# Turning square blocks on VectorE in place of 128x128 transposes on TensorE, in a two-layer decoder trunk

## The chip, the cores and the metric

The kernel runs on one core of a Trainium2 chip. The metric is the device time of one execution in microseconds (us); the number compared is the median of three runs. The profile comes from one further execution, read from the hardware profiler. Five engines work side by side on a core: TensorE (PE; its weight loads are listed as PEld), VectorE (DVE), ScalarE (ACT), GpSimd (POOL) and SyncE (SP), which here only issues transfers.

## The reference, cut to what matters

The input x has 256 tokens of 2048 features, in float32. Two layers follow each other, each a mixer and a feed-forward part, with plain residuals:

```python
h = x
hn = rmsnorm(h, norm_mix[0]);  h = h + s5_mixer(hn, ...)        # state-space mixer, GELU, gated linear unit
hn = rmsnorm(h, norm_ffn[0]);  h = h + swiglu(hn, ...)          # d_ff = 5632
hn = rmsnorm(h, norm_mix[1]);  h = h + sliding_window_attention(hn, ...)
hn = rmsnorm(h, norm_ffn[1]);  h = h + swiglu(hn, ...)
out = rmsnorm(h, norm_final)

def swiglu(x, w_gate, w_up, w_down):
    return (jax.nn.silu(x @ w_gate) * (x @ w_up)) @ w_down
```

A matrix product contracts over features. TensorE contracts over the partitions of its operands. So whatever enters a product as the left operand (the residual h, and the gated values of the feed-forward part) has to be turned first: tokens stand on the partitions where it is computed, and features must stand there where it is used.

## The kernel before, in words

**Products in three parts.** A float32 product is made of three matmuls in a reduced format. Each operand is split into a high part and a low part (the rest), and `products` (L922 to L924) multiplies high by high, high by low and low by high. A `piece` is 512 rows of a weight matrix by 512 columns for both halves of the tokens: 4 x 2 x 3 = 24 matmuls of 128x512. `linear` runs four pieces (2048 features in) or two or three pieces (the down product).

**Weights.** Each piece needs one weight tile of 1 MB. SP's queue loads it into `raw` (two buffers), ScalarE writes its high part (L122), and VectorE its low part (L127). `Weights.next` prepares the tile of two pieces ahead when a piece starts. There are three tiles for split weights, so the high part of piece i+2 can be written when TensorE is done with piece i-1. A `raw` buffer is free, and its next load can start, when the low part is written.

**The residual.** `h` is two tiles of 128 tokens by 2048 features. `Norm.chunk` is called when a chunk of 512 features of h is final; it squares the chunk for the norm and puts a closure into the list `left`. `linear` and `glu` take closures out of that list after each piece, so the turning of a chunk lies among the pieces of the next product.

**Turning.** `normed` turns a chunk of h: eight 128x128 transposes on TensorE into PSUM (L966), then for each of four pairs an activation that scales and writes the high part (L969) and a VectorE instruction for the low part (L970). In `swiglu`, `turned` does the same for a chunk of gated values `act`: eight transposes (L1061), then two casts (L1063) and two subtractions (L1064). There are three norms of h with four chunks each, and two feed-forward parts with eleven chunks of gated values each. The feed-forward part works in groups of chunks: `gu(c)` computes a chunk with eight pieces (four for the gate, four for up), and `down(g)`, twelve pieces for a group of three, comes one chunk later.

**Order.** Engines work through their instructions in the order in which a scheduler put them when the program was built. An engine that waits holds up all that stands behind it in its own list.

Of the kernel before, what the change touches and what calls it, by code (L numbers as in the profile page):

```python
# [17 lines left out]
P = 128  # L18
# [38 lines left out]
def kernel(  # L57
# [9 lines left out]
    def nm(s):  # L67
        uid[0] += 1
        return f"{s}_{uid[0]}"
# [14 lines left out]
    def turned_tile(name):  # L84
        return pp.tile([P, 2, 4, T], F32R, tag="b8", name=nm(name))

    def normed_tile(name):
        return wp.tile([P, 2, 4, T], F32R, tag="xt", name=nm(name), bufs=4)


    class Weights:
        def __init__(self):
            self.src, self.raw, self.hl = [], [], []
            self.early = {}
            self.third = None
            self.used = 0
            self.limit = 0
# [861 lines left out]
    def normed(n, g):  # L959

        o = normed_tile("xT")
        for a in range(4):
            kt = 4 * n + a
            pt = bank([P, 2, P], "tr")
            for t in range(2):
                PE.transpose(pt[:, t], h[t][:, kt * P : (kt + 1) * P], ident)  # L966
            v = pt.rearrange("p t c -> p (t c)")
            gc = gcol[:, g, kt : kt + 1]
            S.activation(o[:, 0, a], v, AF.Copy, scale=gc)  # L969
            V.scalar_tensor_tensor(o[:, 1, a], v, gc, o[:, 0, a].bitcast(F32), ALU.mult, ALU.subtract)  # L970
        return o

    class Norm:


        def __init__(self, g):
            self.g = g
            ssq = wp.tile([P, 32], F32, tag="ssq", name=nm("ssq"), bufs=2)
            self.ssq = ssq[:, : 2 * NCH].rearrange("p (t n) -> p t n", t=2)
            self.xt = [None] * NCH  # L980

        def square(self, n, t):
            junk = wp.tile([P, 512], F32, tag="junk", name=nm("junk"), bufs=2)
            S.activation(
                junk, h[t][:, 512 * n : 512 * n + 512], AF.Square, accum_out=self.ssq[:, t, n : n + 1]
            )

        def chunk(self, n, t):
            self.square(n, t)
            if t == 1:  # L990
                left.append(lambda: self.xt.__setitem__(n, normed(n, self.g)))

        def scale(self):
# [4 lines left out]
    class Last(Norm):  # L998


        def chunk(self, n, t):
            if n == 0 and t == 0:
                self.w = pp.tile([P, D], F32, tag="b8", name="nf")
                nc.scalar.dma_start(self.w, norm_final.unsqueeze(0).to_broadcast([P, D]))
                warm = wp.tile([P, 1], F32, name="warm")
                tc.keep_in_program_order(S.activation(warm, ident[:, 0:1], AF.Sqrt))
            self.square(n, t)
            hc = h[t][:, 512 * n : 512 * n + 512]
# [8 lines left out]
            a, b = slice(0, D // 2), slice(D // 2, D)  # L1017
            V.tensor_scalar(h[t][:, a], h[t][:, a], r, None, ALU.mult)
            nc.sync.dma_start(out[rows, a], h[t][:, a])
            S.activation(h[t][:, D // 2 : D - 512], h[t][:, D // 2 : D - 512], AF.Copy, scale=r)  # L1020
            V.scalar_tensor_tensor(hc, hc, r, wc, ALU.mult, ALU.mult)
            nc.scalar.dma_start(out[rows, b], h[t][:, b])

    def tmp2(name, bufs=4):
        return wp.tile([P, 512], F32, tag=name, name=nm(name), bufs=bufs)

    def glu(norm):
        def load_h(c):
            for t in range(2):
                cs = slice(512 * c, 512 * c + 512)  # L1030
                tc.keep_in_program_order(nc.sync.dma_start(h[t][:, cs], x[t * P : (t + 1) * P, cs]))

        for c in range(NCH):
            left.append(partial(load_h, c))
            if c == 0:
                pa, pb = accs
                for _, half, q in G_ORDER[EARLY:8]:
                    piece(accs[half], gt[q], q == 0, q == 3)
                    if left:
                        left.pop(0)()  # L1040
            else:
                pa = linear(gt)
                pb = linear(gt)
            for t in range(2):
                hc = h[t][:, 512 * c : 512 * c + 512]
                sg = tmp2("act")
                S.activation(sg, pb[t], AF.Sigmoid)
                V.tensor_tensor(sg, pa[t], sg, op=ALU.mult)
                V.tensor_tensor(hc, hc, sg, op=ALU.add)
                norm.chunk(c, t)  # L1050

    def swiglu(norm, out_norm):
        ht = {}
        r = [None]

        def turned(c, hm):
            o = turned_tile("hT")
            for t in range(2):
                pt = bank([P, 4, P], "tr")
                for a in range(4):  # L1060
                    PE.transpose(pt[:, a], hm[t][:, a * P : (a + 1) * P], ident)  # L1061
                ts_ = slice(t * P, (t + 1) * P)
                S.copy(o[:, 0, :, ts_], pt)  # L1063
                V.tensor_tensor(o[:, 1, :, ts_], pt, o[:, 0, :, ts_].bitcast(F32), op=ALU.subtract)  # L1064
            ht[c] = o

        def gu(c):
            pg = linear(norm.xt)
            if r[0] is None:
                r[0] = norm.scale()  # L1070
            sg = []
            for t in range(2):
                s = tmp2("act")
                S.activation(s, pg[t], AF.Silu, scale=r[0][:, t : t + 1])  # L1074
                sg.append(s)
            pu = linear(norm.xt)
            for t in range(2):
                V.scalar_tensor_tensor(sg[t], pu[t], r[0][:, t : t + 1], sg[t], ALU.mult, ALU.mult)
            left.append(lambda: turned(c, sg))

        def down(g):
            xt = Later(ht, FF_GROUPS[g])
            for n in range(NCH):
                last = out_norm.g is None and g == len(FF_GROUPS) - 1 and n == NCH - 1
                acc = linear(xt, len(FF_GROUPS[g]), halves=last)
                for t in range(2):
                    hc = h[t][:, 512 * n : 512 * n + 512]
# [13 lines left out]
    def attention(norm, out_norm):  # L1101
        with tc.tile_pool(name="at", bufs=1) as ap:
# [119 lines left out]
            for c in range(4):  # L1222
                acc = linear(norm.xt)
                b = bias(c)
                tc.keep_in_program_order(S.mul(b, b, HD ** -0.5))
                q = ap.tile([P, 2, 512], F32, tag="q", name=nm("q"), bufs=2)
                for t in range(2):
                    V.scalar_tensor_tensor(q[:, t], acc[t], r8[:, t : t + 1], b, ALU.mult, ALU.add)
                turn_q, scores, turned_s, values = heads(c, q)
                slots.append([turn_q, *late[:1], partial(scores, 0)])  # L1230
                slots.append([*late[1:], partial(scores, 1)])
                slots.append([partial(turned_s, 0)])
                slots.append([partial(values, 0)])
                late = [partial(turned_s, 1), partial(values, 1)]
# [8 lines left out]
            for n in range(NCH):  # L1243
                acc = accs[n] if n < 2 else linear(ot, 4)
                for t in range(2):
                    hc = h[t][:, 512 * n : 512 * n + 512]
                    V.tensor_tensor(hc, hc, acc[t], op=ALU.add)
                    out_norm.chunk(n, t)

# [20 lines left out]

# [27 lines left out]
```

## Time and profile before

| | before |
|---|---|
| median of 3 runs | 2014.27 us (2013.39 to 2014.71) |
| the profiled execution, its own time | 2014.75 us |
| its span in the trace | 2013.0 us |
| TensorE matmuls, busy | 1971.2 us, 98% of the span |
| TensorE weight loads, busy | 1633.5 us, 81% |
| VectorE busy | 1087.0 us, 54% |
| ScalarE busy | 857.9 us, 43% |
| mean busy share of the DMA engines, by stage | 0.54 to 0.68 |

The busy time of an engine is the time in which at least one of its instructions runs. Matmuls overlap at their ends, so a stream of matmuls that start 0.23 us apart and last 0.39 us each counts as fully busy. The 1.75 us between the profiled execution's time and its span lie outside the trace.

### The profile page before, as it was taken

Reading aid. Unit: us, or ns where it says so; the run is one execution under the profiler, and the core shown is the slowest. Engines: PE = TensorE matmul, PEld = TensorE weight load, DVE = VectorE, ACT = ScalarE, POOL = GpSimd, SP = SyncE. Lnnn points to the kernel's source line nnn. Section 1 sums busy time; section 2 is a strip of 40 time slices with the busy share of each in tenths; the row PEclk is TensorE's granted clock in tenths of the full one; section 3 lists DMA queues with packets and bytes.
Section 4 is the critical chain, followed back from the end, with each engine's and each line's share of the span. In section 5 each row is a group of like instructions: output and inputs, shape, how many; then the busy total and the mean of one; then the engine's idle time right before and its main releaser. Section 6 shows DMA issues by size and latency. Waiting matters only on the chain.

```text
span 2013.0 us, 25105 instructions
## 1 busy us (share of the span) xinstructions
PE 1971.2 (98%) x10640; PEld 1633.5 (81%) x10640; DVE 1087.0 (54%) x1343; ACT 857.9 (43%) x871; POOL 103.4 (5%) x77
## 2 busy tenths in 40 slices
PE   7699999999999999999999999999999999999998
PEld 6577888888888888888888888888888888888886
DVE  8964555444444454454566885544454445444445
ACT  6554444333334333433455554433333343343333
POOL 6850000000000000000000000000000000000000
PEclk9899999999999999999999999999999999999999
DMA  4037665565566565555554435566556555655564
GB/s 129 23 109 230 202 202 190 188 188 188 188 189 190 190 198 192 190 188 188 181 196 159 151 126 169 188 189 190 192 192 198 188 188 189 190 190 192 192 198 146
DMA packets 183316, 360.62 MB, mean 179 GB/s; under 512 B 10402, under 2 KB 10466, under 8 KB 183076
## 3 DMA queue, kind: packets, MB, share of 16 engines
q1 hardware_dynamic: 182192, 355.56, 54.8%
q8 instruction: 83, 1.36, 0.3%
q10 hardware_dynamic: 580, 2.14, 0.3%
q0 software_dynamic: 432, 1.33, 0.2%
q14 instruction: 29, 0.24, 0.0%
HBM read 356.90 MB, written 2.10 MB: 178 GB/s over the span
## 4 chain that ended last, share of the span: by engine, by line
PE 93%; DVE 5%; DMA 1%; ACT 1%; issue 0%; POOL 0%; DVEq 0%; ACTq 0%
PE acc L922 29%; PE acc L924 29%; PE acc L923 29%; DVE scan L573 1%; PE tr L1061 1%; DVE V L578 1%; DVE V L576 1%; DMA raw<-in_s_w_glu_dram 1%; DVE w L127 1%; PE pv L210 1%; PE tr L966 1%; PE tr L1196 1%; PE py L798 0%; PE at L1166 0%; PE px L210 0%
## 5 line engine op out<-in xcount | busy, mean ns | idle before, releaser
L127 DVE TENSOR_TENSOR w<-raw,w 128x2048 fp32r<-128x2048 f32 x330 | 757.1, 2294 | 826.3 <-ACT w L122 826.2
L122 ACT ACTIVATE w<-raw 128x2048 fp32r<-128x2048 f32 x332 | 636.2, 1916 | 983.2 <-PE acc L924 834.1
L922 PE MATMUL acc<-w,xT 128*128 128x512 f32 x1568 | 613.1, 391 | 0.0
L924 PE MATMUL acc<-w,xT 128*128 128x512 f32 x1568 | 610.5, 389 | 0.0
L923 PE MATMUL acc<-w,xT 128*128 128x512 f32 x1568 | 610.2, 389 | 0.0
L922 PEld LDWEIGHTS acc<-w,xT 128*128 128x128 f32 x1568 | 294.4, 188 | 62.6 <-issue 2.3
L924 PEld LDWEIGHTS acc<-w,xT 128*128 128x128 f32 x1568 | 294.3, 188 | 61.5
L923 PEld LDWEIGHTS acc<-w,xT 128*128 128x128 f32 x1568 | 294.5, 188 | 60.3
L922 PE MATMUL acc<-w,hT 128*128 128x512 f32 x704 | 275.2, 391 | 0.0
L923 PE MATMUL acc<-w,hT 128*128 128x512 f32 x704 | 273.6, 389 | 0.0
L924 PE MATMUL acc<-w,hT 128*128 128x512 f32 x704 | 273.4, 389 | 0.0
L922 PEld LDWEIGHTS acc<-w,hT 128*128 128x128 f32 x704 | 132.2, 188 | 28.1 <-ACT hT L1063 1.2
L924 PEld LDWEIGHTS acc<-w,hT 128*128 128x128 f32 x704 | 132.1, 188 | 27.6
L923 PEld LDWEIGHTS acc<-w,hT 128*128 128x128 f32 x704 | 132.2, 188 | 27.0
L923 PE MATMUL acc<-w,gt 128*128 128x512 f32 x256 | 99.8, 390 | 0.6 <-DVE w L127 0.6
L922 PE MATMUL acc<-w,gt 128*128 128x512 f32 x256 | 100.1, 392 | 0.0
L924 PE MATMUL acc<-w,gt 128*128 128x512 f32 x256 | 99.7, 389 | 0.0
L923 PEld LDWEIGHTS acc<-w,gt 128*128 128x128 f32 x256 | 48.1, 188 | 10.8 <-DVE w L127 1.0
L1088 DVE TENSOR_TENSOR h<-h,acc 128x512 f32<-128x512 f32 x64 | 43.5, 687 | 24.4 <-PE acc L924 24.4
L924 PEld LDWEIGHTS acc<-w,gt 128*128 128x128 f32 x256 | 48.1, 188 | 10.0
L922 PEld LDWEIGHTS acc<-w,gt 128*128 128x128 f32 x256 | 48.1, 188 | 9.9
L1074 ACT ACTIVATE act<-acc,ry 128x512 f32<-128x512 f32 x44 | 30.1, 690 | 59.9 <-PE acc L924 59.9
(242 smaller groups left out, 1204.6 us busy)
## 6 DMA issues: line engine op xcount, KB each, us to landing
raw<-in_ffn_w_gate_dram SPq DMA_DIRECT2D x88, 1024.0 KB, 5.2
raw<-in_ffn_w_up_dram SPq DMA_DIRECT2D x88, 1024.0 KB, 5.2
raw<-in_ffn_w_down_dram SPq DMA_DIRECT2D x88, 1024.0 KB, 5.1
raw<-in_s_w_glu_dram SPq DMA_DIRECT2D x32, 1024.0 KB, 5.3
raw<-in_attn_w_qkv_dram SPq DMA_DIRECT2D x20, 1024.0 KB, 5.1
raw<-in_attn_w_o_dram SPq DMA_DIRECT2D x16, 1024.0 KB, 5.0
xk<-in_x_dram SPq DMA_DIRECT2D x4, 512.0 KB, 7.1
h<-in_x_dram SPq DMA_DIRECT2D x8, 256.0 KB, 5.8
```

Source lines behind the costliest of these rows:

```text
L122: keep(S.activation(w[:, 0], self.raw[i], AF.Copy))
L127: keep(e.tensor_tensor(lo, self.raw[i], hi.bitcast(F32), op=ALU.subtract))
L210: return (lambda *a, **k: pin(f(*a, **k))) if self.on else f
L573: keep(V.tensor_tensor(t_, ws[..., part], bc(Vt[hf][:, k - 1, :, part], 1, 2), op=ALU.mult))
L576: V.tensor_tensor(v, v, t_[:, 0], op=ALU.add)
L578: V.tensor_tensor(v, v, t_[:, 1, ::-1], op=ALU.add)
L922: keep(PE.matmul(acc, x_[:, 0], w[0][:, a], start=first, stop=False))
L923: PE.matmul(acc, x_[:, 0], w[1][:, a], start=False, stop=False)
L924: PE.matmul(acc, x_[:, 1], w[0][:, a], start=False, stop=last)
L966: PE.transpose(pt[:, t], h[t][:, kt * P : (kt + 1) * P], ident)
L1074: S.activation(s, pg[t], AF.Silu, scale=r[0][:, t : t + 1])
L1088: V.tensor_tensor(hc, hc, acc[t], op=ALU.add)
```

## The change

The residual becomes one tile laid out as [128, chunk, half of the tokens, 512], and the two gated tiles of a chunk become one tile [128, 2, 512]. With that, a chunk is turned by VectorE: `blocks_turned` takes 32 partitions of a chunk (32 tokens of each half) and makes four transposes of 32x32 blocks, each of which writes to another quarter of the partitions of a new tile `bt`. Four calls, 16 VectorE instructions over 32 partitions x 256 elements, turn a chunk. A last closure, `split`, makes the high and low parts from `bt`. For gated values it is one activation and one subtraction over 1024 elements; for h it is four pairs over 256 elements, as before but read from `bt`.

This holds for chunks 0 to 2 of the norm behind the mixer of layer 0 and of the norm behind the attention (`Norm(0, (0, 1, 2))`, `Norm(2, (0, 1, 2))`), and for chunks 0 to 9 of the gated values in each of the two feed-forward parts. Chunk 3 of those two norms, all four chunks of the norm ahead of the attention, and chunk 10 of the gated values are still turned by TensorE. The tile `q` in the attention has one buffer in place of two.

```diff
+    def block_tile():
+        return wp.tile([P, 4, T], F32, tag="bt", name=nm("bt"), bufs=1)
+
+    def blocks_turned(o, v, tb):
+        src = v[32 * tb : 32 * tb + 32].rearrange("p t (a c) -> p t a c", a=4)
+        dst = o.rearrange("p a (t k) -> p t a k", t=2)
+        for q in range(4):
+            V.transpose(dst[32 * q : 32 * q + 32, :, :, 32 * tb : 32 * tb + 32],
+                        src[:, :, :, 32 * q : 32 * q + 32])
...
         def chunk(self, n, t):
             self.square(n, t)
-            if t == 1:
+            if t == 1 and n in self.blocks:
+                o, v = normed_tile("xT"), block_tile()
+                self.xt[n] = o
+                left.extend(partial(blocks_turned, v, h[:, n], tb) for tb in range(4))
+
+                def split():
+                    gc = gcol[:, self.g, 4 * n : 4 * n + 4]
+                    for a in range(4):
+                        S.activation(o[:, 0, a], v[:, a], AF.Copy, scale=gc[:, a : a + 1])
+                        V.scalar_tensor_tensor(o[:, 1, a], v[:, a], gc[:, a : a + 1], o[:, 0, a].bitcast(F32),
+                                               ALU.mult, ALU.subtract)
+
+                left.append(split)
+            elif t == 1:
                 left.append(lambda: self.xt.__setitem__(n, normed(n, self.g)))
...
         def gu(c):
+            last = c == FF_GROUPS[-1][-1]
...
             pu = linear(norm.xt)
             for t in range(2):
-                V.scalar_tensor_tensor(sg[t], pu[t], r[0][:, t : t + 1], sg[t], ALU.mult, ALU.mult)
-            left.append(lambda: turned(c, sg))
+                V.scalar_tensor_tensor(sg[:, t], pu[t], r[0][:, t : t + 1], sg[:, t], ALU.mult, ALU.mult)
+            if last:
+                left.append(lambda: turned(c, sg))
+                return
+            o, v = turned_tile("hT"), block_tile()
+            ht[c] = o
+            left.extend(partial(blocks_turned, v, sg, tb) for tb in range(4))
+
+            def split():
+                S.activation(o[:, 0], v, AF.Copy)
+                V.tensor_tensor(o[:, 1], v, o[:, 0].bitcast(F32), op=ALU.subtract)
+
+            left.append(split)
...
-                q = ap.tile([P, 2, 512], F32, tag="q", name=nm("q"), bufs=2)
+                q = ap.tile([P, 2, 512], F32, tag="q", name=nm("q"))
...
-    h = [wp.tile([P, D], F32, name=f"h{t}") for t in range(2)]
+    h = wp.tile([P, NCH, 2, 512], F32, name="h")
...
-    n0 = Norm(0)
+    n0 = Norm(0, (0, 1, 2))
...
-    n2 = Norm(2)
+    n2 = Norm(2, (0, 1, 2))
```

What stands in the engines' lists is shown at three places, with the rows of before first and those of the change second.

The first place is VectorE behind the up product of one chunk of gated values. `act` is the tile of gated values, written last by L1078 before and by L1102 now; `w` is the low part of a weight tile, and `hT` the low part of the turned chunk.

```order
L1078 SCALAR_TENSOR_TENSOR act_3317<-acc_3320,ry_3307,act_3317 128x512
L127 TENSOR_TENSOR w_3441<-raw_3382,w_3441 128x2048
L127 TENSOR_TENSOR w_3485<-raw_3411,w_3485 128x2048
L1064 TENSOR_TENSOR hT_3470<-tr_3471,hT_3470 128x4x128
L1064 TENSOR_TENSOR hT_3470<-tr_3478,hT_3470 128x4x128
L127 TENSOR_TENSOR w_3514<-raw_3444,w_3514 128x2048
```

```order
L1102 SCALAR_TENSOR_TENSOR act_3586<-acc_3590,ry_3317,act_3586 128x512
L982 STREAM_TRANSPOSE bt_3710<-act_3586 32x2x4x32 x4
L127 TENSOR_TENSOR w_3713<-raw_3652,w_3713 128x2048
L982 STREAM_TRANSPOSE bt_3710<-act_3586 32x2x4x32 x9
L127 TENSOR_TENSOR w_3750<-raw_3681,w_3750 128x2048
L982 STREAM_TRANSPOSE bt_3710<-act_3586 32x2x4x32 x3
L1112 TENSOR_TENSOR hT_3709<-bt_3710,hT_3709 128x1024
L127 TENSOR_TENSOR w_3787<-raw_3716,w_3787 128x2048
```

Sixteen transposes now stand around the next two low parts, and one subtraction of 1024 elements stands in place of two of 512.

The second place is VectorE at the end of the attention, where the chunks 0 and 1 of h become final one after the other (`h`, L1247 before, L1282 now) and are turned for the second feed-forward part (`xT` is the low part of a turned chunk of h).

```order
L1247 TENSOR_TENSOR h_2217<-h_2217,acc_8686 128x512
L1247 TENSOR_TENSOR h_2218<-h_2218,acc_8687 128x512
L127 TENSOR_TENSOR w_9174<-raw_9105,w_9174 128x2048
L127 TENSOR_TENSOR w_9224<-raw_9134,w_9224 128x2048
L970 SCALAR_TENSOR_TENSOR xT_9203<-tr_9204,gcol,xT_9203 128x256
...
L127 TENSOR_TENSOR w_9274<-raw_9177,w_9274 128x2048
```

```order
L1282 TENSOR_TENSOR h<-h,acc_8735 128x512
L1282 TENSOR_TENSOR h<-h,acc_8736 128x512
L982 STREAM_TRANSPOSE bt_9216<-h 32x2x4x32 x4
L127 TENSOR_TENSOR w_9227<-raw_9154,w_9227 128x2048
L982 STREAM_TRANSPOSE bt_9216<-h 32x2x4x32 x6
L127 TENSOR_TENSOR w_9272<-raw_9183,w_9272 128x2048
L1012 SCALAR_TENSOR_TENSOR xT_9215<-bt_9216,gcol,xT_9215 128x256 x4
L982 STREAM_TRANSPOSE bt_9224<-h 32x2x4x32 x8
L127 TENSOR_TENSOR w_9317<-raw_9230,w_9317 128x2048
L982 STREAM_TRANSPOSE bt_9224<-h 32x2x4x32 x8
L127 TENSOR_TENSOR w_9362<-raw_9275,w_9362 128x2048
L1012 SCALAR_TENSOR_TENSOR xT_9223<-bt_9224,gcol,xT_9223 128x256 x4
```

Behind these rows come the addition to h for chunk 2, a low part, ten transposes of chunk 2, a low part and the last six transposes. So three chunks are turned here in two products.

The third place is TensorE in the gated linear unit of layer 0, between the first and the second piece of the second column chunk (`gt` is the turned output of the mixer, `tr` the PSUM tile of a transpose).

```order
L923 MATMUL acc_2351<-w_2280,gt_1731 128x512
L924 MATMUL acc_2351<-w_2280,gt_1731 128x512
L966 MATMUL tr_2382<-ident,h_2217 128x128
L966 MATMUL tr_2382<-ident,h_2218 128x128
...
L966 MATMUL tr_2397<-ident,h_2218 128x128
L922 MATMUL acc_2350<-w_2309,gt_2119 128x512
```

```order
L924 MATMUL acc_2350<-w_2279,gt_1731 128x512
L922 MATMUL acc_2351<-w_2279,gt_1731 128x512
L923 MATMUL acc_2351<-w_2279,gt_1731 128x512
L924 MATMUL acc_2351<-w_2279,gt_1731 128x512
L922 MATMUL acc_2350<-w_2308,gt_2119 128x512
```

The eight transposes between two pieces are gone, and matmul follows matmul. The same holds at 25 other places.

## Rows read from the trace of the kernel before

**Rows 1.** Chain of work that ended last: share of the span by engine.

```profile
PE 93%; DVE 5%; DMA 1%; ACT 1%; issue 0%; POOL 0%; DVEq 0%; ACTq 0%
```

**Rows 2.** Busy time by engine in one stretch, TensorE's clock, DMA share, GB/s.

```profile
348.63:393.08 44.45, 44.45 (x203) 36.88 (x201) 20.97 (x12) 17.55 (x12) 0.00 (x0) 1.00 0.60 189
```

**Rows 3.** The page's costliest groups: busy, mean ns | idle before, and its releaser.

```profile
L127 DVE TENSOR_TENSOR w<-raw,w 128x2048 fp32r<-128x2048 f32 x330 | 757.1, 2294 | 826.3 <-ACT w L122 826.2
L122 ACT ACTIVATE w<-raw 128x2048 fp32r<-128x2048 f32 x332 | 636.2, 1916 | 983.2 <-PE acc L924 834.1
```

**Rows 4.** Timeline of TensorE around one turned chunk: start, us, engine, line.

```profile
348.24 0.40 PE L924 MATMUL acc<-w,xT 128*128 128x512 f32 x1
348.47 1.04 PE L1061 MATMUL tr<-ident,act 128*128 128x128 f32 x8
349.26 0.47 PE L922 MATMUL acc<-w,xT 128*128 128x512 f32 x1
349.58 0.39 PE L923 MATMUL acc<-w,xT 128*128 128x512 f32 x1
```

**Rows 5.** Chain that ended last, in order of time: the turned chunks.

```profile
348.63 0.87 PE tr L1061 x8
393.08 0.88 PE tr L1061 x8
...
481.94 0.87 PE tr L1061 x8
591.63 0.87 PE tr L1061 x8
```

**Rows 6.** Timeline of the first turned chunk of h, TensorE, VectorE and ScalarE.

```profile
168.13 0.39 PE L924 MATMUL acc<-w,gt 128*128 128x512 f32 x1
...
171.56 0.48 PE L922 MATMUL acc<-w,gt 128*128 128x512 f32 x1
...
170.68 2.28 DVE L127 TENSOR_TENSOR w<-raw,w 128x2048 fp32r<-128x2048 f32 x1
...
178.46 1.92 ACT L122 ACTIVATE w<-raw 128x2048 fp32r<-128x2048 f32 x1 [2.96 <-DMA raw<-in_s_w_glu_dram]
```

**Rows 7.** Groups by form, VectorE and ScalarE: the nearest to what is new.

```profile
L970 DVE SCALAR_TENSOR_TENSOR xT<-tr,gcol,xT 128x256 fp32r<-128x256 f32 x48 | 19.9, 476 | 2.0 <-ACT xT L969 2.0
L1216 DVE TENSOR_TENSOR oT<-po,oT 128x256 fp32r<-128x256 f32 x16 | 6.1, 409 | 0.0
L1187 DVE TENSOR_SCALAR sc<-sc,sm 128x256 f32<-128x256 f32 x32 | 11.2, 349 | 0.0
L1064 DVE TENSOR_TENSOR hT<-tr,hT 128x512 fp32r<-128x512 f32 x44 | 28.2, 682 | 0.0
L210 ACT ACTIVATE U<-xk 128x1024 f32<-128x1024 f32 x4 | 4.3, 1082 | 0.0
```

**Rows 8.** Timeline of VectorE and ScalarE behind one chunk of gated values.

```profile
1318.46 1.43 DVE L1078 SCALAR_TENSOR_TENSOR act<-acc,ry,act 128x512 f32<-128x512 f32 x2 [0.52 <-PE acc L924]
1321.08 2.29 DVE L127 TENSOR_TENSOR w<-raw,w 128x2048 fp32r<-128x2048 f32 x1 [1.20 <-ACT w L122]
1326.53 2.29 DVE L127 TENSOR_TENSOR w<-raw,w 128x2048 fp32r<-128x2048 f32 x1 [3.15 <-ACT w L122]
...
1319.13 1.92 ACT L122 ACTIVATE w<-raw 128x2048 fp32r<-128x2048 f32 x1 [3.52 <-PE acc L924]
```

**Rows 9.** DMA issues of the gate weights: KB each, us to landing.

```profile
raw<-in_ffn_w_gate_dram SPq DMA_DIRECT2D x88, 1024.0 KB, 5.2
```

**Rows 10.** Timeline at the end of the attention, VectorE and ScalarE.

```profile
1227.78 1.37 DVE L1247 TENSOR_TENSOR h<-h,acc 128x512 f32<-128x512 f32 x2 [0.52 <-PE acc L924]
...
1238.06 1.65 DVE L970 SCALAR_TENSOR_TENSOR xT<-tr,gcol,xT 128x256 fp32r<-128x256 f32 x4
...
1233.90 1.92 ACT L122 ACTIVATE w<-raw 128x2048 fp32r<-128x2048 f32 x1 [2.26 <-PE acc L924]
1240.24 1.92 ACT L122 ACTIVATE w<-raw 128x2048 fp32r<-128x2048 f32 x1 [2.97 <-PE acc L924]
```

More of the change, by code (lines that the diff above doesn't have):

```diff
@@ L965, in normed @@
             for t in range(2):
-                PE.transpose(pt[:, t], h[t][:, kt * P : (kt + 1) * P], ident)
+                PE.transpose(pt[:, t], h[:, n, t, a * P : (a + 1) * P], ident)
             v = pt.rearrange("p t c -> p (t c)")
@@ L971, in normed, with __init__ @@
         return o
+    def block_tile():
[6 more added lines that the diff above has]
+                        src[:, :, :, 32 * q : 32 * q + 32])
     class Norm:
-        def __init__(self, g):
-            self.g = g
+        def __init__(self, g, blocks=()):
+            self.g, self.blocks = g, blocks
             ssq = wp.tile([P, 32], F32, tag="ssq", name=nm("ssq"), bufs=2)
@@ L984, in square @@
             S.activation(
-                junk, h[t][:, 512 * n : 512 * n + 512], AF.Square, accum_out=self.ssq[:, t, n : n + 1]
+                junk, h[:, n, t], AF.Square, accum_out=self.ssq[:, t, n : n + 1]
             )
@@ L1007, in chunk @@
             self.square(n, t)
-            hc = h[t][:, 512 * n : 512 * n + 512]
+            hc = h[:, n, t]
             wc = self.w[:, 512 * n : 512 * n + 512]
@@ L1016, in chunk @@
             rows = slice(t * P, (t + 1) * P)
[L1017 to L1020, printed above, removed]
+            a, b = h[:, :2, t], h[:, 2:, t]
+            o = out[rows].rearrange("p (n c) -> p n c", n=NCH)
+            V.tensor_scalar(a, a, r, None, ALU.mult)
+            nc.sync.dma_start(o[:, :2], a)
+            S.activation(b[:, 0], b[:, 0], AF.Copy, scale=r)
             V.scalar_tensor_tensor(hc, hc, r, wc, ALU.mult, ALU.mult)
-            nc.scalar.dma_start(out[rows, b], h[t][:, b])
-    def tmp2(name, bufs=4):
-        return wp.tile([P, 512], F32, tag=name, name=nm(name), bufs=bufs)
+            nc.scalar.dma_start(o[:, 2:], b)
     def glu(norm):
@@ L1030, in load_h @@
                 cs = slice(512 * c, 512 * c + 512)
-                tc.keep_in_program_order(nc.sync.dma_start(h[t][:, cs], x[t * P : (t + 1) * P, cs]))
+                tc.keep_in_program_order(nc.sync.dma_start(h[:, c, t], x[t * P : (t + 1) * P, cs]))
         for c in range(NCH):
@@ L1043, in glu @@
                 pb = linear(gt)
+            act = wp.tile([P, 2, 512], F32, tag="act", name=nm("act"), bufs=2)
             for t in range(2):
-                hc = h[t][:, 512 * c : 512 * c + 512]
-                sg = tmp2("act")
+                hc = h[:, c, t]
+                sg = act[:, t]
                 S.activation(sg, pb[t], AF.Sigmoid)
@@ L1060, in turned @@
                 for a in range(4):
-                    PE.transpose(pt[:, a], hm[t][:, a * P : (a + 1) * P], ident)
+                    PE.transpose(pt[:, a], hm[:, t, a * P : (a + 1) * P], ident)
                 ts_ = slice(t * P, (t + 1) * P)
@@ L1070, in gu @@
                 r[0] = norm.scale()
-            sg = []
+            sg = wp.tile([P, 2, 512], F32, tag="act", name=nm("act"), bufs=2)
             for t in range(2):
-                s = tmp2("act")
-                S.activation(s, pg[t], AF.Silu, scale=r[0][:, t : t + 1])
-                sg.append(s)
+                S.activation(sg[:, t], pg[t], AF.Silu, scale=r[0][:, t : t + 1])
             pu = linear(norm.xt)
             for t in range(2):
-                V.scalar_tensor_tensor(sg[t], pu[t], r[0][:, t : t + 1], sg[t], ALU.mult, ALU.mult)
-            left.append(lambda: turned(c, sg))
+                V.scalar_tensor_tensor(sg[:, t], pu[t], r[0][:, t : t + 1], sg[:, t], ALU.mult, ALU.mult)
[9 more added lines that the diff above has]
+            left.append(split)
         def down(g):
@@ L1086, in down @@
                 for t in range(2):
-                    hc = h[t][:, 512 * n : 512 * n + 512]
+                    hc = h[:, n, t]
                     V.tensor_tensor(hc, hc, acc[t], op=ALU.add)
@@ L1245, in attention @@
                 for t in range(2):
-                    hc = h[t][:, 512 * n : 512 * n + 512]
+                    hc = h[:, n, t]
                     V.tensor_tensor(hc, hc, acc[t], op=ALU.add)
```

## The prediction

> **What bounds the kernel now.** I read the chain of work that ended last first: TensorE holds 93% of the span [rows 1]. So the question for every part of the change is whether it lengthens or shortens TensorE's stream. Next come the groups with their idle time. VectorE spends 757 us on low parts of weights, and ahead of them it idles 826 us, released by ScalarE; ScalarE in turn idles ahead of the high parts, mostly until TensorE lets go of a weight tile [rows 3]. The reader is to see a loop in which TensorE sets the pace and the two other engines wait for it. The busy time of one stretch says the same: in 44.45 us TensorE is busy for all of it at a granted clock of 1.00, VectorE for 20.97 us, ScalarE for 17.55 us, and the DMA engines have a share of 0.60 [rows 2]. What is taken out of TensorE's stream is therefore gained, as long as the other three keep up.
>
> **What is removed: TensorE's time.** The transposes stand between matmuls without a gap. One chunk's eight lie between a matmul that starts at 348.24 and one that starts at 349.26; the one after follows at 349.58 [rows 4]. Two steps of the stream take 1.34 us there. The normal step comes from the chain: two successive chunks of gated values are turned 44.45 us apart with eight pieces between them, and 109.69 us apart with eight pieces and the twelve of a down product [rows 5]. So twelve pieces take 65.24 us, a piece 5.44 us, a matmul 0.227 us. The block costs 1.34 - 0.45 = 0.89 us by the matmuls' starts, and 44.45 - 8 x 5.44 = 0.93 to 0.96 us by the chain. I take 0.92 us. There are 26 such blocks: 10 chunks of gated values in each of two feed-forward parts and three chunks in each of two norms. The first block of all costs more. There the transposes are the first to need h, which VectorE has yet to add up, and TensorE stands from its matmul at 168.13 to the next at 171.56 [rows 6]: 3.43 - 0.23 = 3.2 us. Sum: 25 x 0.92 + 3.2 = 26.2 us.
>
> At one place a rule of the notes is set against this. The Trainium skill, page "VectorE: DVE Perf Modes", section "Rules for kernel authors", advises TensorE for a 128x128 transpose whose result may go to PSUM, and its section "The three transpose paths" gives 390 ns for one on TensorE and 311 ns on VectorE, for 16-bit data and within 32x32 blocks only. By that 390 ns, eight transposes would hold TensorE 3.1 us and the gain would be some 81 us; the row has 0.92 us for the eight, since they overlap in a stream, and the sum goes by the row.
>
> **What is added on VectorE.** Per chunk there are 16 transposes over 32 partitions x 256 elements, 416 in all. The trace has none, so their price d is bounded by rows of 256 elements: 349 ns for an operation of one source from SBUF, 409 ns for one of two sources, 476 ns with a scalar per partition [rows 7]. A lower end is 0.33 us, if neighbours overlap a little as four L970 do, which take 1.65 us together instead of 4 x 0.476 [rows 7, 10]. The upper end is 0.68 us, the row over 512 elements, as if an element of four bytes took two steps [rows 7]. I take 0.42 us, nearest to the rows with the same count of elements. VectorE's total then grows by 416 x 0.42 = 175 us, to some 63% of the span. The low part of a gated chunk changes from 2 x 0.682 us to one of 1024 elements, 1.22 us between the rows of 512 and 2048 elements [rows 3, 7]; ScalarE's high part becomes one of 1024 elements, 1.08 us [rows 7]. The instructions on h keep their count and size. So only the transposes weigh, and where they stand decides. The cover is VectorE's idle time and the lead of the weights.
>
> **Is the lead long enough behind a gated chunk?** A high part starts when a piece starts, and its tile is used two pieces later. For the high part at 1319.13 the low part is due at 1319.13 + 2 x 5.44 = 1330.0; the third low part behind the gated values, two pieces on, is due at 1319.13 + 4 x 5.44 = 1340.9 [rows 8]. VectorE is done with the gated values at 1319.89. From there the list holds 4 transposes, a low part, 9 transposes, a low part, 3 transposes; then ScalarE copies 1.08 us, and only behind that does it write the third high part, 1.92 us, which the third low part, 2.29 us, waits for. In sum 1319.9 + 16 d + 2 x 2.29 + 1.08 + 1.92 + 2.29 = 1329.8 + 16 d, against 1340.9: it holds up to d = 0.69. With 0.42 the slack is 4.4 us. The `raw` buffers: a low part frees one, and the load behind it lands 5.2 us later [rows 9]. Today the low part that starts at 1321.08 ends at 1323.4, the load lands at 1328.6, and ScalarE takes it up two pieces behind 1319.13, at 1330.0: 1.4 us to spare. With d = 0.42 the three low parts end 0.4, 1.0 and 1.3 us later than today, which stays inside it. I cost these twenty chunks at nothing.
>
> **At the end of the attention** three chunks are turned in two products, and this is the tightest place. From 1227.78 VectorE's list up to the low part behind the first ten transposes of chunk 2 holds 36 transposes, two pairs of additions (2 x 1.37), six low parts (6 x 2.29) and eight instructions on h (2 x 1.65) [rows 3, 10]: 19.8 + 36 d. Without transposes the high parts start 5.44 us apart instead of the 6.34 us that rows show here, so that low part's high part starts at 1233.90 + 4 x 5.44 = 1255.7 and it is due at 1266.5. The window is 38.7 us, which holds up to d = 0.52. With 0.42 the slack is 3.8 us: nothing.
>
> **At the start** ScalarE still waits for weights to land (2.96 us at 178.46), and low parts are made about 5 us ahead of need [rows 6]. TensorE now arrives 3.2 us earlier, and two groups of eight transposes, 3.4 us each, stand ahead of low parts. I take 0.7 us off, and 3.2 us at most, when TensorE is back at its old schedule.
>
> **Other edits** are free: the squares, additions and outputs over the new layout of h have the same count and size, `q` with one buffer is read one product before it is written again, and eight banks of PSUM only lose users.
>
> **Sum.** 26.2 - 0.7 = 25.5 us. The profiled execution took 2014.75 us (span 2013.0), 0.5 us over the median of the runs; less 25.5 it gives 1989.2, and 1988.8 against the median. I predict 1989.
>
> **The rivals.**
> - *A, the forecast:* d between 0.33 and 0.5, all covered; 1986.5 to 1991. Chance 0.75.
> - *B, the bursts are not covered:* the sixteen transposes write to four quarters of the partitions in turn and run strictly one after another, at 0.52 to 0.69 us each. Against it: the rows of 256 elements have 0.35 to 0.48 us. At d = 0.6 the end of the attention is 19.8 + 36 x 0.6 - 38.7 = 2.7 us late, and about twice that by the last six; the start gives back up to 3.2 us. That is 4 to 8 us: 1993 to 1998. Chance 0.13. The Trainium skill, page "VectorE: DVE Perf Modes", section "Two Vector instructions with no wait between them", has a rule for it: an instruction whose output starts in another group of 32 partitions than the last one's is held until all earlier ones are done. Each of the sixteen would be held by that rule; no run here shows it yet. It alone takes away the overlap and gives 0.41 to 0.48 us, which still fits; B needs a longer transpose besides.
> - *C, slower:* the transposes take over 0.69 us, and VectorE is late for weights behind each gated chunk. The stall is 16 (d - 0.69) for each of 20 chunks, and at the end of the attention 36 (d - 0.52). At d = 0.73 these are 13 and 8 us, which with 3 us at the start is nearly the whole gain, and it decides from there; at d = 1.0 they are 99 and 17 us: 2014 - 26 + 99 + 17 + 3 = 2107. For it speaks that nothing in the trace shows a transpose of four-byte elements on VectorE, against it that every row of 256 elements is below 0.48 us. Chance 0.07.
> - *D, the loads fall behind:* low parts made later free `raw` later, and a round of 5.2 + 1.92 + 2.29 = 9.4 us against two pieces of 10.9 us has only 1.5 us for it. If landings lengthen with it, half the gain is lost: 2001. Against it: rounds without transposes follow and recover. Chance 0.05.
>
> **How the numbers follow.** The likeliest is A, 1989. The range takes in A, B and D, from 1985.5 (all 26.2 us, and a lower price of the blocks' edges) to 2001, and leaves out C. Within 0.2% (4 us), which is about what a measurement of this kernel can tell from no change, lie only a few values of d near 0.72. So faster 0.91, same 0.02, slower 0.07.
>
> **What would show it.** Matmuls 0.227 us apart with no gap where a chunk is turned; eight pieces of a gated chunk in 43.5 us where 44.45 stood; TensorE busy some 24 us less; STREAM_TRANSPOSE x416 at 0.35 to 0.48 us; idle time of VectorE ahead of L127 down by some 170 us, and no wait of TensorE for `w`. The forecast is wrong if TensorE waits for VectorE's low parts, first between 1240 and 1270 us or behind a gated chunk, or if a matmul's step grows.

## The result, and the profile after

| | before | with the change |
|---|---|---|
| median | 2013.98 us (4 runs) | 1989.94 us (4 runs) |
| lowest to highest | 2013.39 to 2014.71 | 1988.56 to 1991.19 |
| the profiled execution, its own time | 2014.75 us | 1990.07 us |
| its span in the trace | 2013.0 us | 1988.3 us |

The ratio is 0.9879, with a 95% interval of 0.9865 to 0.9893: 24.0 us less. The forecast was 1989.

The page of the changed kernel, its busy times, its chain by engine and four of its groups (columns as in [rows 3]):

```profile
PE 1950.3 (98%) x10432; PEld 1613.8 (81%) x10432; DVE 1267.0 (64%) x1739; ACT 861.0 (43%) x851; POOL 103.4 (5%) x77
...
PE 93%; DVE 4%; DMA 1%; ACT 1%; issue 0%; POOL 0%; DVEq 0%; ACTq 0%
...
L127 DVE TENSOR_TENSOR w<-raw,w 128x2048 fp32r<-128x2048 f32 x330 | 757.9, 2297 | 600.3 <-ACT w L122 598.3
L122 ACT ACTIVATE w<-raw 128x2048 fp32r<-128x2048 f32 x332 | 636.3, 1916 | 845.8 <-PE acc L924 578.6
...
L982 DVE STREAM_TRANSPOSE bt<-act 32x256 f32<-32x256 f32 x320 | 139.6, 436 | 5.5
...
L1111 ACT ACTIVATE hT<-bt 128x1024 fp32r<-128x1024 f32 x20 | 21.2, 1062 | 106.6 <-DVE bt L982 106.6
```

TensorE still holds 93% of the chain [rows 1]. VectorE is 180 us busier and still has 600 us of idle time ahead of the low parts, where it had 826 [rows 3]. ScalarE now waits 106.6 us for the last transposes ahead of `hT`; these waits cost nothing, since TensorE doesn't wait behind them.

One gated chunk of the changed kernel, as a stretch (columns as in [rows 2]), and TensorE's timeline in it:

```profile
342.00:385.48 43.48, 43.48 (x193) 36.03 (x192) 27.94 (x28) 17.66 (x11) 0.00 (x0) 1.00 0.61 193
```

```profile
341.79 0.39 PE L922 MATMUL acc<-w,xT 128*128 128x512 f32 x1
342.01 0.39 PE L923 MATMUL acc<-w,xT 128*128 128x512 f32 x1
342.24 0.39 PE L924 MATMUL acc<-w,xT 128*128 128x512 f32 x1
342.47 0.39 PE L922 MATMUL acc<-w,xT 128*128 128x512 f32 x1
```

TensorE is busy for the whole stretch at a clock of 1.00, in steps of 0.227 us; VectorE has 27.94 us of 43.48, where it had 20.97 of 44.45 [rows 2].

The chain in order of time, five of the blocks that TensorE still turns (chunk 3 of the first norm, chunk 10 of the first feed-forward part, chunk 1 of the norm ahead of the attention, then chunk 3 and chunk 10 in the second layer):

```profile
300.26 0.87 PE tr L966 x8
975.72 0.87 PE tr L1086 x8
...
999.65 0.88 PE tr L966 x8
...
1264.31 0.87 PE tr L966 x8
1939.76 0.87 PE tr L1086 x8
```

From chunk 3 of h to gated chunk 10 it takes 675.46 us in the first layer and 675.45 us in the second: both feed-forward parts run alike, to a hundredth of a microsecond.

### The profile page after: what moved, and what is told of

Its sections match the earlier page's. It is cut to its first block, busy times and chain, and to the rows that moved or that the text cites. A ratio compares the mean times of both kernels' runs of the same rounds, so it can differ in the third digit from the quotient of the medians.

```text
span 1988.3 us, 25061 instructions
## 1 busy us (share of the span) xinstructions
PE 1950.3 (98%) x10432; PEld 1613.8 (81%) x10432; DVE 1267.0 (64%) x1739; ACT 861.0 (43%) x851; POOL 103.4 (5%) x77
## 4 chain that ended last, share of the span: by engine, by line
PE 93%; DVE 4%; DMA 1%; ACT 1%; issue 0%; POOL 0%; DVEq 0%; ACTq 0%
PE acc L922 30%; PE acc L923 30%; PE acc L924 30%; DVE scan L573 1%; DMA raw<-in_s_w_glu_dram 1%; DVE w L127 1%; DVE V L578 1%; DVE V L576 1%; PE pv L210 1%; PE tr L1231 1%; PE py L798 0%; PE at L1201 0%; PE pm L754 0%; ACT w L122 0%; PE at L1200 0%
## 5 line engine op out<-in xcount | busy, mean ns | idle before, releaser
L982 DVE STREAM_TRANSPOSE bt<-act 32x256 f32<-32x256 f32 x320 | 139.6, 436 | 5.5
L1111 ACT ACTIVATE hT<-bt 128x1024 fp32r<-128x1024 f32 x20 | 21.2, 1062 | 106.6 <-DVE bt L982 106.6
L923 PEld LDWEIGHTS acc<-w,gt 128*128 128x128 f32 x256 | 48.1, 188 | 11.5 <-DVE w L127 1.7
L922 PEld LDWEIGHTS acc<-w,gt 128*128 128x128 f32 x256 | 48.1, 188 | 9.9
```

Source lines behind the costliest of these rows:

```text
L922: keep(PE.matmul(acc, x_[:, 0], w[0][:, a], start=first, stop=False))
L923: PE.matmul(acc, x_[:, 0], w[1][:, a], start=False, stop=False)
L982: V.transpose(dst[32 * q : 32 * q + 32, :, :, 32 * tb : 32 * tb + 32], src[:, :, :, 32 * q : 32 * q + 32])
L1111: S.activation(o[:, 0], v, AF.Copy)
```

## The experiments

Each diff is against the changed kernel.

**The layout alone.** All chunks are turned by TensorE; the one tile for h, the one for two gated values and the single buffer of `q` stay.

```diff
-            last = c == FF_GROUPS[-1][-1]
+            last = True
...
-    n0 = Norm(0, (0, 1, 2))
+    n0 = Norm(0)
-    n2 = Norm(2, (0, 1, 2))
+    n2 = Norm(2)
```

> All chunks are turned by TensorE again; the single tile of h, the joined tile of gated values and the one buffer of q stay. Theory (the gain is TensorE's time of the removed transposes and nothing else): the time of the kernel before, 2014 within 2 us. Rival (part of the gain comes from the new layout of h or of the gated values, through fewer waits or coarser tiles): 2003 to 2010.

Measured: 2014.75 us, ratio 1.0004 (0.9995 to 1.0013). The layout is free, and the whole gain belongs to who does the turning.

**The gated chunks alone, and the chunks of h alone.** In the first run only the lines of `Norm` above are set back, in the second only `last`.

> Only the 20 chunks of gated values are turned by VectorE, the chunks of h by TensorE. Theory: 20 blocks of 0.92 us, 18.4 us less than before: 1995.6, and TensorE still stands some 2 us ahead of its first transposes of h. Rival (bursts behind a gated chunk already cost TensorE time, and the chunks of h bring more than their blocks): 1998 to 2004.

> Only the six chunks of h are turned by VectorE. Theory: 5 blocks of 0.92 us and 3.2 us at the first one, less up to 1 us for late weights at the start: 7 us less than before, 2007, of which 2.8 us lie at the end of the attention. Rival (the bursts at the end of the attention or at the start are not covered): 2009 to 2014, with TensorE waiting for w there.

Measured: 1996.52 us for the gated chunks (0.9914, 0.9897 to 0.9931) and 2007.02 us for h (0.9965, 0.9952 to 0.9978). These are 17.5 and 7.0 us less than before; together 24.4, against 24.0 for the change. The interval of the first reaches to 2000.1 us, into its rival's range, so there the trace decides: behind 165 us TensorE waits for no low part in either run. The two parts add up within the noise, so neither is seen to use the other's cover.

**The transposes of h made twice.** What is written is the same; VectorE's bursts on h become twice as long (`times` is 2 for h and 1 for gated values).

```diff
+            for _ in range(times):
                 V.transpose(dst[32 * q : 32 * q + 32, :, :, 32 * tb : 32 * tb + 32],
                             src[:, :, :, 32 * q : 32 * q + 32])
```

> Each transpose of a chunk of h is made twice in a row (the same data to the same place), those of gated values once. Theory (a transpose costs nothing until VectorE's list overruns the lead of the weights, which was 0.52 us per transpose at the end of the attention): with 0.448 us from start to start the doubled bursts overrun. At the end of the attention the list up to the fourth low part is 26 us of transposes, 9.2 of low parts and 3 of the rest against a window of 27.9 us, 10 us late, and two more groups of 16 transposes in a piece each add 4 us: some 18 us of waits of TensorE for w. At the start 7 to 10 us. In sum 2012 to 2020. Rival (TensorE does not depend on VectorE's lead here, waits go elsewhere): 1990 to 1994.

Measured: 2030.10 us (1.0080, 1.0065 to 1.0095), some 10 us over the range expected. The waits themselves, 15.3 us at the end of the attention and 11.3 us at the start, are near to what was expected; what was left out is shown below. **The gated chunks' transposes made twice** is the same edit for the other part:

> Each transpose of gated values is made twice in a row, those of h once. The list behind a gated chunk is then 4, low part, 12, low part, 16, low part, and only then the copy and the subtraction. Theory: up to the third low part 14.3 us of transposes and 6.9 us of low parts start when the gated values are done; with the window of 21.0 us that is 0.2 us late for each of 20 chunks, and the copy of ScalarE behind it holds up the next high part: 1990 to 2000. Rival (the lead is as the prediction put it, used up at 0.69 us per transpose): 16 x (0.90 - 0.69) = 3.3 us for each of 20 chunks, 2056. Rival (no cost at all while VectorE has idle time left in a round): 1990 within 1.5.

Measured: 2039.41 us (1.0120, 1.0103 to 1.0137), outside all three ranges. The waits of TensorE for low parts (us in all, times, longest), then span and mean granted clock, of the run with h twice:

```profile
PE acc L923 <- DVE w L127: 27.2, 9, 7.7
```

```profile
core 0: 2028.1 us, clock 0.986
```

The same two views of the run with the gated chunks twice:

```profile
PE acc L923 <- DVE w L127: 29.4, 22, 3.6
```

```profile
core 0: 2038.8 us, clock 0.984
```

The waits explain 27 and 29 us of the 40.2 and 49.5 us that were lost against the changed kernel (0.6 us of each lies ahead of 160 us and stands in the changed kernel too). The rest is mostly TensorE's clock, which the expectations had left out. Here is one wait in the run with the gated chunks twice, as TensorE's timeline and as stretches behind it:

```profile
404.93 0.39 PE L922 MATMUL acc<-w,xT 128*128 128x512 f32 x1
408.63 0.80 PE L923 MATMUL acc<-w,xT 128*128 128x512 f32 x1 [3.32 <-DVE w L127]
409.23 0.63 PE L924 MATMUL acc<-w,xT 128*128 128x512 f32 x1
409.65 0.63 PE L922 MATMUL acc<-w,xT 128*128 128x512 f32 x1
```

```profile
410.00:412.00 2.00, 2.00 (x6) 1.53 (x5) 1.92 (x1) 0.30 (x1) 0.00 (x0) 0.50 0.91 305
412.00:414.00 2.00, 2.00 (x6) 1.52 (x6) 0.00 (x0) 0.28 (x1) 0.00 (x0) 0.50 0.90 244
414.00:418.00 4.00, 4.00 (x18) 3.29 (x17) 2.29 (x1) 2.31 (x2) 0.00 (x0) 0.94 0.63 241
```

Behind the wait the matmuls start 0.43 us apart instead of 0.227, at a granted clock of 0.50, until shortly after 414 us. The mean clock gives the size of it: a clock of 0.984 over 2038.8 us is 32.6 us at full speed not granted, and 28.4 us with h twice, against 0.992 over 1988.3 us, 15.9 us, in the changed kernel. That is 16.7 and 12.5 us more, each to about 1 us, since the clock has three digits. The three traces have the same 10432 matmuls, so their steps from start to start can also be set side by side, from the matmul at 170 us on. The run with the gated chunks twice falls 50.7 us behind the changed kernel: 31.9 us in 20 steps that hold a wait, 15.2 us in the other steps at the lower clock, and 3.6 us in small delays. With h twice it is 39.9 us: 27.9 us in eight steps with a wait, 11.4 us at the lower clock, and 0.6 us.

Why the waits come is seen in the timelines of VectorE and ScalarE in the run with the gated chunks twice, around the first two gated chunks, and in ScalarE's waits there (us in all, times, longest):

```profile
338.26 1.43 DVE L1103 SCALAR_TENSOR_TENSOR act<-acc,ry,act 128x512 f32<-128x512 f32 x2 [0.52 <-PE acc L924]
...
359.16 2.29 DVE L127 TENSOR_TENSOR w<-raw,w 128x2048 fp32r<-128x2048 f32 x1
...
388.73 2.29 DVE L127 TENSOR_TENSOR w<-raw,w 128x2048 fp32r<-128x2048 f32 x1 [1.40 <-ACT w L122]
...
377.22 1.92 ACT L122 ACTIVATE w<-raw 128x2048 fp32r<-128x2048 f32 x1 [4.87 <-DMA raw<-in_ffn_w_gate_dram]
...
386.78 1.92 ACT L122 ACTIVATE w<-raw 128x2048 fp32r<-128x2048 f32 x1 [4.96 <-DMA raw<-in_ffn_w_gate_dram]
```

```profile
ACT w L122 <- DMA raw<-in_ffn_w_down_dram: 155.4, 53, 5.2
...
ACT w L122 <- DMA raw<-in_ffn_w_gate_dram: 136.3, 45, 5.0
```

The row of the down weights in the changed kernel:

```profile
ACT w L122 <- DMA raw<-in_ffn_w_down_dram: 53.0, 17, 4.9
```

At the first chunk the third low part ends at 361.45, and TensorE waits for it 0.62 us. From the end of the gated values (339.69) the formula gives 32 x 0.448 + 3 x 2.29 = 21.2 us, against a window of 21.0; the trace has 21.8 us, since in this run the transposes start 0.46 us apart. At the second chunk the wait is 3.32 us. A low part that should follow the first four transposes at once stands 1.40 us for ScalarE, which waits for a load. Behind the first chunk ScalarE waits for a load each time, and the load until VectorE frees its `raw` buffer. ScalarE takes weights out of one of the two buffers at 377.22 and 386.78, a round of 9.6 us, where two pieces last 10.9 us. So a round makes up little more than 1 us, and the next burst comes before the lead is back. ScalarE's waits for down weights are 155.4 us in all. The overrun of one chunk is small, but the lead is not refilled by the next chunk.

**A burst of 24.** Of each gated chunk's 16 transposes, 8 are made twice (`more` is true for gated values alone).

```diff
+            for _ in range(1 + (more and q % 2)):
                 V.transpose(dst[32 * q : 32 * q + 32, :, :, 32 * tb : 32 * tb + 32],
                             src[:, :, :, 32 * q : 32 * q + 32])
```

> Of the 16 transposes of a chunk of gated values 8 are made twice, so 24 stand where 16 stood, in all twenty chunks; h is as in the change. Theory (the window behind a gated chunk decides, and a chunk that fits it costs nothing): up to the third low part 23 transposes stand, 23 x 0.448 + 6.9 = 17.2 us against a window of 21.0 us, so TensorE has no wait for w in the two feed-forward parts and the time stays at 1990 us, within 1.5. Rival (what broke the run with 32 was not the window but a lead that isn't refilled: each burst that is longer than the idle time behind it carries a rest into the next chunk): VectorE does 24 x 0.448 = 10.8 us more per chunk than in the kernel before, the loads fall behind, and the time is 1995 us or more with waits of TensorE for w that grow from chunk to chunk.

Measured: 1989.34 us (0.9875, 0.9860 to 0.9889). VectorE's groups of this run, low parts and transposes:

```profile
L127 DVE TENSOR_TENSOR w<-raw,w 128x2048 fp32r<-128x2048 f32 x330 | 757.6, 2296 | 544.5 <-ACT w L122 542.0
L983 DVE STREAM_TRANSPOSE bt<-act 32x256 f32<-32x256 f32 x480 | 209.5, 436 | 11.0
```

160 transposes more, 70 us of VectorE, cost nothing, and TensorE waits for no low part behind 160 us. So the cover is real and its edge lies between 24 and 32 transposes, where the window puts it for one chunk by itself: (21.0 - 6.9) / 0.448 = 31. The rival's time is wrong, but what it says of a rest that is carried on is seen. With low parts and pieces matched one by one, the third low part behind the gated values is done 3.5, 3.2, 2.6 and 2.5 us ahead of the matmul that needs it at the first four chunks, which follow each other closely, and 3.5 us again behind the down product. With 16 transposes it is 3.9 us at each of the twenty chunks.

**Each transpose cut in two.** Two instructions of 32x128 write one quarter one after the other, then come the next two.

```diff
+            for t in range(2):
-                V.transpose(dst[32 * q : 32 * q + 32, :, :, 32 * tb : 32 * tb + 32],
-                            src[:, :, :, 32 * q : 32 * q + 32])
+                V.transpose(dst[32 * q : 32 * q + 32, t, :, 32 * tb : 32 * tb + 32],
+                            src[:, t, :, 32 * q : 32 * q + 32])
```

> Each transpose is cut into two over 128 elements, 32 per chunk; the second of a pair reads and writes in the same groups of 32 partitions as the first. If a transpose moves one element per step and has a fixed part, 436 ns = fixed + 256 x 1.04 gives a fixed part of 0.17 us, so 0.30 us for one of 128 elements; if it is held back only where the group of 32 partitions changes, the pairs start closer than they last. Theory: 32 x 0.27 to 0.30 us = 8.6 to 9.6 us for a chunk against 7.2; the end of the attention then is 0.54 to 0.60 us per old transpose, 1 to 3 us over its window, the rest is hidden: 1990 to 1995. Rival (a transpose is all fixed cost): 0.44 us each, time as in the doubled runs, over 2005.

Measured: 1990.93 us (0.9886, 0.9871 to 0.9901), no different from the change by the intervals. TensorE has one wait for a low part more than there, 0.4 us at the end of the attention, where 1 to 3 us were expected. Its group on the page, and a burst in its timeline of VectorE:

```profile
L983 DVE STREAM_TRANSPOSE bt<-act 32x128 f32<-32x128 f32 x640 | 160.3, 282 | 5.0
```

```profile
1309.62 4.37 DVE L983 STREAM_TRANSPOSE bt<-act 32x128 f32<-32x128 f32 x17
```

Seventeen halves take 4.37 us, 0.257 us each, while one lasts 0.282 us on average. Instruction by instruction, the second of a pair starts 0.24 us behind a first that lasts 0.30 us; the next pair starts 0.27 us behind a second that lasts 0.26 us. So halves that stay in one quarter overlap. The whole ones do not (below).

**More chunks for VectorE.** The norm ahead of the attention has its chunks turned by VectorE too: chunks 0 to 2, then chunk 0 alone, then chunk 0 with its five closures put one behind each piece, in a list of their own, where the change takes them out of `left` as fast as that list is served.

```diff
-    n1 = Norm(1)
+    n1 = Norm(1, (0, 1, 2))
```

> Chunks 0 to 2 of the norm ahead of the attention are turned by VectorE too. They come in the last down product, where a chunk of h is final after every two pieces (10.9 us). Theory: VectorE needs 1.4 + 2 x 2.3 + 16 x 0.448 + 1.7 = 14.8 us for each, 3.9 us more than there is; three of them overrun by 11.7 us, of which a lead of some 6.5 us is covered, and 2.8 us of TensorE's time are saved: 2 to 3 us slower than the changed kernel, 1992 to 1994. Rival (VectorE catches up as at the end of the attention): 1987.2.

```diff
-    n1 = Norm(1)
+    n1 = Norm(1, (0,))
```

> Only chunk 0 of the norm ahead of the attention is turned by VectorE too. Theory: one overrun of 3.9 us is inside the lead of the weights, and one block of 0.92 us is saved: 1989.0. Rival (it delays what stands behind it in the last down product): 1990 to 1992.

```diff
+            if spread:
+                spread.pop(0)()
...
-                left.extend(partial(blocks_turned, v, h[:, n], tb) for tb in range(4))
+                late = spread if self.g == 1 else left
+                late.extend(partial(blocks_turned, v, h[:, n], tb) for tb in range(4))
...
-                left.append(split)
+                late.append(split)
...
-    n1 = Norm(1)
+    n1 = Norm(1, (0,))
```

> Chunk 0 of h in the norm ahead of the attention is turned by VectorE too, as in the run with one chunk there, but its four groups of transposes and its last step are each put behind another piece instead of behind one another, so that the additions to h for chunk 1 don't stand behind all sixteen. Theory (the 1.7 us wait of TensorE for h in that run came from the order on VectorE alone): no wait of the transposes on TensorE for h, and 0.92 us less than the changed kernel: 1989.0 us. Rival (VectorE is too full in that stretch whatever the order): the wait stays at 1 us or more, 1990.5 to 1991.5 us. The difference of 0.05% is at the edge of what five rounds can tell, so the waits decide.

Measured: 1992.88 us with three chunks (0.9897, 0.9882 to 0.9912), 1990.78 with one (0.9885, 0.9870 to 0.9900), 1988.69 with one spread out (0.9873, 0.9857 to 0.9890). These intervals overlap with that of the change, so the waits decide. With three chunks TensorE waits for low parts twice behind 160 us, 4.1 us in all, more than three blocks give. With one chunk it waits elsewhere; TensorE and then VectorE in its timeline:

```profile
998.13 0.39 PE L924 MATMUL acc<-w,hT 128*128 128x512 f32 x1
1000.22 1.26 PE L966 MATMUL tr<-ident,h 128*128 128x128 f32 x8 [1.70 <-DVE h L1123]
```

```profile
990.27 5.39 DVE L982 STREAM_TRANSPOSE bt<-h 32x256 f32<-32x256 f32 x12
...
999.49 1.28 DVE L1123 TENSOR_TENSOR h<-h,acc 128x512 f32<-128x512 f32 x2
```

Chunk 1 is still turned by TensorE, and its transposes need h, whose addition stands on VectorE behind the twelve transposes of chunk 0, a low part and four instructions on `xT`. So the block saved comes back as a wait of 1.7 us. Spread out, the wait is gone; the chain's blocks in that run:

```profile
974.74 0.87 PE tr L1090 x8
997.75 0.87 PE tr L969 x8
```

These two blocks lie 23.01 us apart; in the changed kernel chunk 10 and chunk 1 lie 23.93 apart (975.72 and 999.65), so 0.92 us is gained there, a block's price, as the theory had it. The times of the two kernels can't be told apart by their intervals; this stretch can.

## Why the prediction was right, step by step

**What bounds the kernel: right.** Behind 160 us the changed kernel's trace has one wait of TensorE for a low part, 0.26 us, and none for anything else (the start, below).

**A block costs 0.92 us: right.** From chunk 3 of h to gated chunk 10 it was 684.55 us (304.22 to 988.77) and is 675.46: 9.09 us for ten blocks. VectorE's last step on the gated values runs ahead of the kernel before by 3.95 us at the first chunk and by 13.05 us at the eleventh, 0.89 to 0.93 us more from chunk to chunk. From chunk 3 of the first norm to the end of the span it was 1708.8 us (304.22 to 2013.0) and is 1688.0 us: 20.7 us for 23 blocks, against 21.2.

**The first block, 3.2 us, less 0.7 for late weights: the second number was too large.** Between the end of the first column chunk's matmuls and chunk 3 of h it was 136.1 us (168.13 to 304.22) and is 131.4 (168.88 to 300.26): 4.7 us, where 3.2 + 2 x 0.92 - 0.7 = 4.3 was forecast. The wait that is left there stands in TensorE's timeline:

```profile
169.10 0.39 PE L922 MATMUL acc<-w,gt 128*128 128x512 f32 x1
169.59 0.50 PE L923 MATMUL acc<-w,gt 128*128 128x512 f32 x1
```

The step is 0.49 us instead of 0.227: 0.26 us in place of 0.7. But this, and not the end of the attention, was the tightest place: the next three low parts are done only 1.0, 0.7 and 0.2 us ahead of the matmul that needs them.

**The price of a transpose, 0.42 us with 0.33 to 0.68: right, at 0.448.** VectorE behind a gated chunk of the second feed-forward part, the answer to [rows 8]:

```profile
1302.63 1.43 DVE L1102 SCALAR_TENSOR_TENSOR act<-acc,ry,act 128x512 f32<-128x512 f32 x2 [0.52 <-PE acc L924]
1304.10 1.79 DVE L982 STREAM_TRANSPOSE bt<-act 32x256 f32<-32x256 f32 x4
1305.92 2.29 DVE L127 TENSOR_TENSOR w<-raw,w 128x2048 fp32r<-128x2048 f32 x1
1308.24 4.03 DVE L982 STREAM_TRANSPOSE bt<-act 32x256 f32<-32x256 f32 x9
...
1314.62 1.35 DVE L982 STREAM_TRANSPOSE bt<-act 32x256 f32<-32x256 f32 x3
1317.09 1.23 DVE L1112 TENSOR_TENSOR hT<-bt,hT 128x1024 fp32r<-128x1024 f32 x1 [1.13 <-ACT hT L1111]
1318.90 2.29 DVE L127 TENSOR_TENSOR w<-raw,w 128x2048 fp32r<-128x2048 f32 x1 [0.58 <-ACT w L122]
```

Nine take 4.03 us: 0.448 from start to start, for a duration of 0.436. So rival B's mechanism holds (strictly one after another), but not its price of 0.52 us and more, and rival C's 0.69 is far away. The third low part ends at 1321.19. From the end of the gated values, 1304.06, that is 17.1 us, and the formula's 9.9 + 16 x 0.448 = 17.1; the window is 21.0. The matmul that needs this low part starts 3.9 us after it is done, as the difference says.

**The window at the end of the attention: right, and nearly used up.** VectorE runs there without a pause, the answer to [rows 10]:

```profile
1215.71 1.28 DVE L1282 TENSOR_TENSOR h<-h,acc 128x512 f32<-128x512 f32 x2
...
1249.05 2.29 DVE L127 TENSOR_TENSOR w<-raw,w 128x2048 fp32r<-128x2048 f32 x1
...
1259.73 2.29 DVE L127 TENSOR_TENSOR w<-raw,w 128x2048 fp32r<-128x2048 f32 x1 [1.76 <-ACT w L122]
```

The low part behind the first ten transposes of chunk 2 ends at 1251.34, 35.6 us after the start; 19.8 + 36 x 0.448 = 35.9 was the sum, 38.7 the window. TensorE does not wait; the low part is done 2.2 us ahead of need. With h turned twice the list has another order, and 74 transposes stand ahead of the same low part. It ends 53.1 us after the start of the additions (1234.56 to 1287.67), and the formula gives 19.8 + 74 x 0.448 = 53.0, 14.3 us over the window. TensorE's waits up to there are 10.9 us; the matmuls at the lower clock in between delay it too. A wait of 4.4 us more comes with the last sixteen transposes.

**The loads: the slack was smaller than forecast, and it cost nothing.** The prediction had the loads behind a gated chunk's low parts land in time, with 1.4 us to spare. In the trace ScalarE waits for two of them there (1.02 us at 1319.88, 0.69 us at 1326.45), and its waits for weights of the feed-forward parts are 121.6 us in all, where the kernel before has 9.1. TensorE has no wait from it. Rival D takes over only in the run with 32 transposes.

**VectorE's idle time ahead of the low parts** was to fall by some 170 us and fell by 226: VectorE is 180 us busier, and the span is 25 us shorter.

**The 0.9 us by which the forecast was too low** lie within the spread of the runs (1988.56 to 1991.19). By the trace the change gives 4.7 + 20.7 = 25.4 us (25.5 were forecast). That the two are so close is partly luck: 0.4 us more than forecast at the start and 0.5 us less behind it cancel. Before any chunk is turned, the profiled execution is 0.75 us behind (168.88 against 168.13). That part varies: the same addition to h of the first column chunk starts here in the profiles of the changed kernel and of the layout alone:

```profile
170.65 1.29 DVE L1074 TENSOR_TENSOR h<-h,act 128x512 f32<-128x512 f32 x2
```

```profile
168.22 1.28 DVE L1074 TENSOR_TENSOR h<-h,act 128x512 f32<-128x512 f32 x2
```

In the profiles of all eleven kernels with the new layout it lies between these two, 2.4 us apart, though the edits lie behind it. From there also comes most of why TensorE's busy time fell by 20.9 us and not by 24: from 60 to 120 us the mean granted clock is 0.83 in this profile against 0.89 in that of before, and TensorE is busy for 46.5 us against 43.3.

## What to carry to other kernels

Where one engine's stream sets the time, price what leaves it by its steps in the stream (0.92 us for eight transposes), and what another engine takes over by the window it falls into: the longest burst ahead of the next thing that engine owes. Here the window was an edge: 24 transposes cost as little as 16, and 32 cost 49 us, since the lead was not won back and some waits were paid again in the clock. Counts in between were not tried. Look also at what else is queued behind the burst; in one place, handing it out one piece at a time took away a wait of 1.7 us and gave the 0.92 us that the block was worth.

## What the runs showed of the hardware that was not expected

**Transposes on VectorE into changing quarters do not overlap.** Whole ones (32x256, four bytes) start 0.448 us apart and last 0.436 us. Halves (32x128), of which every second stays in the quarter of the one before, start 0.257 us apart and last 0.282 us. The Trainium skill, page "VectorE: DVE Perf Modes", section "Two Vector instructions with no wait between them", says that an instruction whose output starts in another group of 32 partitions than the last one's is held until the earlier ones are done; both runs agree with that. The runs with transposes made twice are no test of it: many of those carry semaphore waits, which the changed kernel's don't, and start 0.46 us apart. Since a pair of halves takes 0.514 us, one whole transpose is still the cheaper.

**A wait of TensorE can be paid again.** Behind a wait of 3.32 us the granted clock was 0.50, which is 1.2 of 2.4 GHz, and 14 matmuls from 408.63 to 414.66 took 6.03 us instead of 3.18. With h twice, one of 1.83 us was followed by a mean of 0.52 from 1252.6 to 1255.8. Behind the wait of 1.70 us of the run with one more chunk the clock stayed at 1.00, and so it did behind one of 2.82 us in the run with the gated chunks twice (1.00 from 1399.3 to 1402.5). So not each such wait is paid twice, its length alone doesn't decide it, and what does was not tried.
